# Gate and up of two feed-forward layers as 2x2-block products with seven multiplications in half of their k-groups

## The chip, the cores and the metric

The kernel runs on one core of a Trainium2 chip. The metric is the device time of one execution in microseconds (us). Every matmul operand is float32, split into two float32r parts (high and low), and each product is made of three matmuls: high x high, high x low and low x high.

## What is computed

Two transformer blocks over 256 tokens of width 2048. The change touches their feed-forward layers (FFN), of 5632 hidden columns:

```python
h = h + jnp.concatenate([oa, ob, oc], axis=-1) @ w_out[i]
c = rmsnorm(h, ffn_norm[i])
h = h + conv_ffn(c, w_gate[i], w_up[i], conv_w[i], conv_b[i], w_down[i])
...
x = x + mixed
h = rmsnorm_2(x, ffn_norm_w[l])
x = x + (jax.nn.silu(h @ w_gate[l]) * (h @ w_up[l])) @ w_down[l]
```

`conv_ffn` runs a causal convolution of width 3 along the tokens over the gate's output, adds a bias, takes a gelu and multiplies by the up output, before `w_down`.

## The kernel before

Tokens are two tiles of 128 rows (m = 0, 1). The activations lie transposed as stationary operands: for each of the 16 k-tiles a pair of 128x256 tiles (`xT`, high and low). Weights are the moving operand, in blocks of two k-tiles by 512 columns (128x1024, 512 KB), one block a k-group; `KG` is 2, so a 2048-deep product has eight k-groups.

`load_weight` (L102) gets a block by DMA into one of seven raw buffers (three of tag `raw`, four of tag `t4k`). `split_weight` (L128) makes its parts: ScalarE copies it to `whi` (L133), VectorE subtracts `whi` from the raw block to give `wlo` (L134). `whi` and `wlo` are rings of three buffers. `product` (L158 is the last of its three matmul lines, L156 to L158) runs over the k-groups: a split, then for two k-tiles and two m three matmuls each, 12 in all, into two PSUM banks of tag `acc`. PSUM has four banks of tag `acc` and four of tag `tp`.

An FFN works in units of 512 hidden columns, u = 0 to 10. A unit is `product` with the gate weight and `product` with the up weight, 96 matmuls each; `evacuate` (L236) moves each from PSUM to a `pj` tile of 1024 columns (ring of eight) with the token's factor r. `hidden` turns a unit's result into four pairs of stationary `hid` tiles: transposes on TensorE (L195), then, in the first FFN, five operations on ScalarE and VectorE (L569 to L573) and the split (L184, L185); in the second FFN only the split. These steps are side work: generators in a list, of which `pump` runs up to two steps after each k-group of a product, so that they stand between its matmuls. `ffn` takes units in groups of two, (0, 1) to (8, 9) and (10). After both units of a group the group before is drained: for each of four chunks of 512 columns of h, `product` with the down weight over the group's eight hidden tiles (48 matmuls), then `add_to_h`, two VectorE additions of the banks to h (L544). The last group of the second FFN goes to `final_rows`.

A scheduler orders each engine's row of instructions when the program is built, from the order of the code and its own costs. What stands in `tc.high_priority()`, as the splits do, is put as early as its buffers allow. It also gives out the buffers of a tag. Each engine then runs its row in that order, and an instruction that waits holds all behind it.

`norm_chunk` transposes a chunk of h, scales it by the norm's weights and splits it into `xT`; the token's factor r is applied after the products. In the second block's attention `mod_weights` gets for each head a bias row from DRAM (`vdr`) into one of two `mbias` buffers, after the scores, and adds it there (L838).

Of the kernel before, what the change touches and what calls it, by code (L numbers as in the profile page):

```python
# [17 lines left out]
P = 128  # L18
T = 256
# [34 lines left out]
def two_blocks_kernel(ctx: ExitStack, tc: tile.TileContext, A: dict, out: bass.AP):  # L54
# [87 lines left out]
    def add_side(gen, after=0):  # L142
        side.append([tick[0] + after, gen])
# [54 lines left out]
    def norm_chunk(c, g, st):  # L198

        for kk in range(4):  # L200
            if kk == 2:
                yield 1
            k = c * 4 + kk
            t = transpose_pair([h[c][:, m, kk * P : (kk + 1) * P] for m in range(2)])
            st.xs[k] = stationary(t, "xT", g[:, k : k + 1])
        for m in range(2):
            junk = t2k()
            act(junk, h[c][:, m], AF.Square, accum_out=st.ssq[:, m, c : c + 1])
        if c == NCH - 1:
# [16 lines left out]
    def token_r(st):  # L226
# [4 lines left out]
        pool.tensor_tensor(st.r, ms, mhalf[:, :2], op=ALU.pow)  # L231

# [313 lines left out]
    def residual_norm(w, xin, g, order=None):  # L546

        st = NormState()
# [6 lines left out]
    xs, r = residual_norm(W["out"], mix, G_FFN)  # L555


    def conv_unit(u, xs, r):
        gt = evacuate(product(W["gate"], u, xs), r)
        ut = evacuate(product(W["up"], u, xs), r)  # L560
# [34 lines left out]
    def ffn(unit, down, xs, r, g):  # L595
        groups = [(0, 1), (2, 3), (4, 5), (6, 7), (8, 9), (10,)]
        prev = None
        st = NormState() if g is not None else None

        def drain(u0, hid, last):  # L600
            if last and g is None:
                return final_rows(down, u0, hid)
            for c in range(NCH):
# [11 lines left out]
        drain(*prev, True)  # L615
        return (st.xs, st.r) if g is not None else None
# [59 lines left out]
    def gla_gate(dd):  # L676
        lrt = new([17, T], "lrt", 2)
# [136 lines left out]

    def mod_weights(all_pts, hp):
        (qc, qo), (kc, ko) = mod_at(hp, 0), mod_at(hp, 1)
        qT, kT = t1k(), t1k()
# [12 lines left out]
        for a in range(2):  # L830
            hh = hp * 2 + a
            bt = new([P, 384], "mbias", 2)
            row = vdr[hh : hh + 1, :]
            nc.sync.dma_start(bt, bass.AP(row.tensor, row.offset, [[1, P], [1, 384]]))
# [59 lines left out]
    xs, r = residual_norm(W["out2"], mix, G_FFN2, order=[4, 5, 6, 7, 0, 1, 2, 3])  # L894


    def final_rows(down, u0, hid):
# [3 lines left out]
        tags = [("pj", 8)] * 8 + [("t4k", 4)] * 4 + [("whi", 3)] * 2 + [("wlo", 3)] * 2  # L901
# [150 lines left out]
```

## Time and profile before

| | |
|---|---|
| Median of 3 runs | 2465.67 us (2463.63 to 2466.41) |
| The profiled execution | 2463.04 us |
| Its span in the profile | 2461.1 us, 30001 instructions |
| TensorE, matmuls | 11424, busy 2436.0 us |
| TensorE, weight loads | 11424, busy 2016.2 us |
| VectorE | 1767 instructions, busy 1421.1 us |
| ScalarE | 1705 instructions, busy 1219.0 us |
| DMA | 448.86 MB, mean 182 GB/s |

In a view of the trace a row names the engine (PE is TensorE, PEld its weight loads, DVE VectorE, ACT ScalarE, SP the queue of the DMAs), the line of the code, the operation, and output<-input by the program's tile names with partitions x elements. In square brackets stands how long the engine had been idle before, and what ended it. A matmul's record is longer than the distance to the next one's start, since they are pipelined.

### The profile page before, as it was taken

To read this page: it belongs to the slowest core of one execution; us is meant where nothing else is said; L and a number is where in the kernel's file an instruction comes from. 1 tells how busy PE (TensorE), PEld (TensorE's weight loads), DVE (VectorE), ACT (ScalarE), POOL (GpSimd) and SP (SyncE) were. 2 spreads that over 40 slices of the span, in tenths; PEclk is the share of its full clock that TensorE was granted. 3 is DMA by queue.
4 is the path that set the end of the run, shared out by engine and by line. 5 is a ranking of instruction groups with operands and counts; after the bars stand their busy time and mean duration, and the time that the engine had idled before them with its cause. 6 is when DMAs were issued, how large, how long until landed. Compare 5 with 4: busy or idle time off the path is not lost.

```text
span 2461.1 us, 30001 instructions
## 1 busy us (share of the span) xinstructions
PE 2436.0 (99%) x11424; PEld 2016.2 (82%) x11424; DVE 1421.1 (58%) x1767; ACT 1219.0 (50%) x1705; POOL 20.5 (1%) x26
## 2 busy tenths in 40 slices
PE   8999999999999999999999999999999999999998
PEld 7878888888888888888887888788888888888887
DVE  6686565555556465555656755655545545454556
ACT  6545454455445454544556555654444444434444
POOL 0000000000000000000000000000000000000000
PEclk9999999999999999999999999999999999999999
DMA  7444565555555655555545455555555555555554
GB/s 239 142 144 153 179 205 185 188 187 181 188 190 186 194 182 190 187 188 187 184 150 181 149 198 187 166 162 182 192 189 191 192 189 189 191 192 189 189 195 143
DMA packets 130654, 448.86 MB, mean 182 GB/s; under 512 B 14860, under 2 KB 19852, under 8 KB 130510
## 3 DMA queue, kind: packets, MB, share of 16 engines
q1 hardware_dynamic: 130510, 446.95, 56.2%
q8 instruction: 89, 1.46, 0.2%
q14 instruction: 55, 0.45, 0.1%
HBM read 444.76 MB, written 2.13 MB: 182 GB/s over the span
## 4 chain that ended last, share of the span: by engine, by line
PE 94%; DVE 2%; DMA 1%; issue 1%; ACT 1%; POOL 0%; SPq 0%; POOLq 0%; DVEq 0%; ACTq 0%
PE acc L158 30%; PE acc L156 30%; PE acc L157 29%; PE tp L195 2%; DVE wlo L134 1%; DMA mbias<-vdr 1%; ACT whi L133 0%; PE tp L361 0%; DMA raw<-in_w_down 0%; DMA raw<-in_w_in 0%; PE tp L863 0%; DVE t2k L838 0%; DVE at L370 0%; PE tp L848 0%; DMA h<-in_x 0%
## 5 line engine op out<-in xcount | busy, mean ns | idle before, releaser
L156 PE MATMUL acc<-whi,xT 128*128 128x512 f32 (+3 forms) x2400 | 936.4, 390 | 0.0
L158 PE MATMUL acc<-whi,xT 128*128 128x512 f32 (+3 forms) x2400 | 923.9, 385 | 0.0
L157 PE MATMUL acc<-wlo,xT 128*128 128x512 f32 (+3 forms) x2400 | 923.8, 385 | 0.0
L134 DVE TENSOR_TENSOR wlo<-raw,whi 128x1024 fp32r<-128x1024 f32 (+3 forms) x483 | 575.0, 1191 | 520.0 <-ACT whi L133 519.2
L133 ACT ACTIVATE whi<-raw 128x1024 fp32r<-128x1024 f32 (+3 forms) x483 | 498.9, 1033 | 587.6 <-PE acc L158 526.0
L134 DVE TENSOR_TENSOR wlo<-t4k,whi 128x1024 fp32r<-128x1024 f32 x353 | 432.7, 1226 | 437.0 <-ACT whi L133 436.8
L133 ACT ACTIVATE whi<-t4k 128x1024 fp32r<-128x1024 f32 x353 | 374.3, 1060 | 478.4 <-PE acc L158 458.3
L158 PEld LDWEIGHTS acc<-whi,xT 128*128 128x128 f32 x2400 | 451.1, 188 | 91.0 <-issue 0.9
L156 PEld LDWEIGHTS acc<-whi,xT 128*128 128x128 f32 x2400 | 451.4, 188 | 87.5 <-issue 2.9
L157 PEld LDWEIGHTS acc<-wlo,xT 128*128 128x128 f32 x2400 | 452.0, 188 | 85.6 <-issue 0.4
L156 PE MATMUL acc<-whi,hid 128*128 128x512 f32 x944 | 373.6, 396 | 0.0
L157 PE MATMUL acc<-wlo,hid 128*128 128x512 f32 x952 | 370.8, 389 | 0.0
L158 PE MATMUL acc<-whi,hid 128*128 128x512 f32 x944 | 368.4, 390 | 0.0
L158 PEld LDWEIGHTS acc<-whi,hid 128*128 128x128 f32 x944 | 177.2, 188 | 38.2
L157 PEld LDWEIGHTS acc<-wlo,hid 128*128 128x128 f32 x952 | 179.0, 188 | 35.6
L156 PEld LDWEIGHTS acc<-whi,hid 128*128 128x128 f32 x944 | 177.3, 188 | 35.3 <-issue 0.4
L236 ACT ACTIVATE pj<-acc,r 128x512 f32<-128x512 f32 (+3 forms) x96 | 63.4, 662 | 41.1 <-PE acc L158 41.1
L544 DVE TENSOR_TENSOR h<-h,acc 128x512 f32<-128x512 f32 x104 | 67.1, 680 | 0.0
L195 PE MATMUL tp<-ident,pj 128*128 128x128 f32 x344 | 54.4, 272 | 1.3 <-DVE t2k L838 1.3
L195 PEld LDWEIGHTS tp<-ident,pj 128*128 128x128 f32 x344 | 43.5, 140 | 14.4 <-DVE t2k L838 1.8
L416 ACT ACTIVATE t2k<-t2k,col 128x256 f32<-128x256 f32 (+1 forms) x56 | 26.9, 480 | 23.6 <-DVE col L415 23.5
L184 ACT ACTIVATE hid<-t1k 128x256 fp32r<-128x256 f32 x44 | 18.3, 416 | 35.6 <-DVE t1k L573 35.6
(229 smaller groups left out, 1082.9 us busy)
## 6 DMA issues: line engine op xcount, KB each, us to landing
raw<-in_w_in SPq DMA_DIRECT2D x184, 512.0 KB, 3.5
t4k<-in_w_gate SPq DMA_DIRECT2D x100, 512.0 KB, 3.4
t4k<-in_w_up SPq DMA_DIRECT2D x100, 512.0 KB, 3.4
t4k<-in_w_down SPq DMA_DIRECT2D x96, 512.0 KB, 3.4
raw<-in_w_down SPq DMA_DIRECT2D x80, 512.0 KB, 3.5
raw<-in_w_gate SPq DMA_DIRECT2D x76, 512.0 KB, 3.5
raw<-in_w_up SPq DMA_DIRECT2D x76, 512.0 KB, 3.5
t4k<-in_w_out SPq DMA_DIRECT2D x37, 512.0 KB, 3.5
```

The lines of the kernel that those rows point to most:

```text
L133: act(hi[:, :n], raw[:, :n], AF.Copy)
L134: dve.tensor_tensor(lo[:, :n], raw[:, :n], hi[:, :n].bitcast(F32), op=ALU.subtract)
L156: pe.matmul(o, xhi[:, tok], wh, start=first, stop=False)
L157: pe.matmul(o, xhi[:, tok], wl, start=False, stop=False)
L158: pe.matmul(o, xlo[:, tok], wh, start=False, stop=last)
L184: act(hi, src, AF.Copy)
L195: pe.transpose(t[:, m * P : (m + 1) * P], v, ident)
L236: act(t[:, m, :n], acc[m][:, :n], func, scale=r[:, m : m + 1])
L416: act(lg[:, a:b], lg[:, a:b], AF.Exp, bias=nm[:, m : m + 1], accum_out=sm[:, m : m + 1])
L544: dve.tensor_tensor(h[c][:, m], h[c][:, m], acc[m], op=ALU.add)
```

## The change

Call X the normalized activations and take the weights of gate (a) and up (b) side by side. For a pair of k-groups gp and gp + 4 and the two token tiles, gate and up are a 2x2-block product: b11, b12 are the blocks of gate and up in k-group gp, b21, b22 those in gp + 4. In gp = 0 and 2 of units 2 to 10 (`MIXED`) the eight block products are replaced by seven, in Winograd's form of Strassen's scheme. In gp = 1 and 3, and in units 0 and 1, the eight are kept.

- Weight side: t1 = b11 + b12, t3 = b12 + b22, t2 = t1 + b22, t4 = t2 + b21, each a VectorE addition of 128x1024 written in place into a raw buffer. Split are b11, b21, b22, t1, t3, t2, t4 (`split_raw`): seven where there were four. Each split then feeds six matmuls instead of 12.
- Activation side: `strassen_operands` makes four factors for each of the four k-tiles concerned, once an FFN, as side work; they stay in four of the eight `pj` tiles.
- PSUM: `pair_product` uses all eight banks: p1, q5, p2, q3 of tag `acc`, and q6, q7, x22, q4 of tag `tp`. Beside the fourth group p1, q5, q6 and q7 are combined in two `pj` tiles (ca, cb), and at the end p2, q3, q4 and x22 are added.
- Side work doesn't run inside `pair_product`. `ffn` drains two chunks after each unit instead of four after two units.
- The rings `whi` and `wlo` have five buffers instead of three.
- `norm_chunk` scales the rows of h by the previous norm's factor (rho) before the transposes, where one is given, and r is divided by it.
- `mod_bias` loads the second attention's bias rows at the start of `mod_weights`, into four buffers.

```diff
-        hi, lo = tiles or (new([P, KG * 512], "whi", 3, F32R), new([P, KG * 512], "wlo", 3, F32R))
+        hi, lo = tiles or (new([P, KG * 512], "whi", 5, F32R), new([P, KG * 512], "wlo", 5, F32R))
...
+        if st.rho is not None:
+            rows = [t2k(), t2k()]
+            for m in range(2):
+                act(rows[m], h[c][:, m], AF.Copy, scale=st.rho[:, m : m + 1])
...
+    def strassen_operands(xs):
...
+                    for t, (hi, lo) in ((a, xs[k]), (b, xs[k + 8])):
+                        dve.tensor_tensor(t, hi.bitcast(F32), lo.bitcast(F32), op=ALU.add)
...
+                    dve.tensor_tensor(d, a21, a22, op=ALU.subtract)
+                    dve.tensor_tensor(s2, d, a11, op=ALU.subtract)
+                    dve.tensor_tensor(s3, a11, a21, op=ALU.subtract)
+                    dve.tensor_tensor(s4, s2, a12, op=ALU.add)
+                    x = chunk_tile(F32R)
+                    act(x[:, 0], fm, AF.Copy)
+                    dve.tensor_tensor(x[:, 1], fm, x[:, 0].bitcast(F32), op=ALU.subtract)
...
+    def pair_product(wa, wb, u, xs, sx):
+        p1, q5, p2, q3 = (psum("acc") for _ in range(4))
+        q6, q7, x22, q4 = (psum() for _ in range(4))
+        ca, cb = chunk_tile(), chunk_tile()
...
+        for gp in range(half):
+            if gp not in MIXED:
+                for w_, banks in ((wa, (p2, q4)), (wb, (q3, x22))):
+                    for g in (gp, gp + half):
+                        wt = split_weight(w_, u, g)
+                        for m in range(2):
+                            products(banks[m], plain(g, m), wt, g == KT // KG - 1)
+                continue
+            last = gp == MIXED[-1]
+            b11, b12, b21, b22 = (load_weight(w_, u, g) for g in (gp, gp + half) for w_ in (wa, wb))
+            with tc.high_priority():
+                f11 = split_raw(b11)
+                t1 = b11
+                dve.tensor_tensor(t1, b11, b12, op=ALU.add)
+                f21 = split_raw(b21)
+                f22 = split_raw(b22)
+                t3 = b12
+                dve.tensor_tensor(t3, b12, b22, op=ALU.add)
+            products(p1, plain(gp, 0), f11, last)
+            products(p2, plain(gp + half, 0), f21, gp == half - 1)
+            products(q3, mixed(gp, 3), f22, gp == half - 1)
...
+            products(q5, mixed(gp, 0), ft1, last)
+            products(q7, mixed(gp, 2), ft3, last)
...
+            products(q6, mixed(gp, 1), ft2, last)
...
+            products(q4, plain(gp + half, 1), ft4, gp == half - 1)
+            if last:
+                act(ca[:, 0], p1, AF.Copy)
+                dve.tensor_tensor(ca[:, 1], ca[:, 0], q6, op=add)
+                dve.scalar_tensor_tensor(cb[:, 0], ca[:, 1], -1.0, q5, ALU.mult, add)
+                dve.tensor_tensor(ca[:, 1], ca[:, 1], q7, op=add)
+                dve.tensor_tensor(cb[:, 1], cb[:, 0], q7, op=sub)
+
+        for t, bank in ((ca[:, 0], p2), (cb[:, 0], q3), (ca[:, 1], q4), (cb[:, 1], x22)):
+            dve.tensor_tensor(t, t, bank, op=add)
...
-                add_side(fill(hid, 4 * i, unit(u, xs, r)))
-            if prev is not None:
-                drain(*prev, False)
+                add_side(fill(hid, 4 * i, unit(u, xs, r, sx if u > 1 else None)))
+                if prev is not None:
+                    step = NCH // len(us)
+                    drain(*prev, range(i * step, (i + 1) * step))
...
     def mod_weights(all_pts, hp):
         (qc, qo), (kc, ko) = mod_at(hp, 0), mod_at(hp, 1)
+        bts = [mod_bias(hp * 2 + a) for a in range(2)]
```

What the scheduler made of it, at three places, as rows of an engine (line, operation, output<-inputs). The first is VectorE where the first FFN enters unit 4. Before, the drain's last additions to h stand among splits of the down weight and of the unit's gate weight:

```order
L544 TENSOR_TENSOR h_4_69<-h_4_69,acc_5659 128x512
L134 TENSOR_TENSOR wlo_5775<-t4k_5772,whi_5774 128x1024
L134 TENSOR_TENSOR wlo_5793<-t4k_5790,whi_5792 128x1024
L134 TENSOR_TENSOR wlo_5815<-raw_5812,whi_5814 128x1024
L134 TENSOR_TENSOR wlo_5833<-raw_5830,whi_5832 128x1024
L544 TENSOR_TENSOR h_5_70<-h_5_70,acc_5734 128x512
L544 TENSOR_TENSOR h_5_70<-h_5_70,acc_5735 128x512
```

Now, after the last split of the drain's second chunk; L604 is a split in `split_raw`, L648, L652, L659 and L662 make t1, t3, t2 and t4, L556 is the addition to h, and L700 to L703 and L185 belong to hidden blocks:

```order
L556 TENSOR_TENSOR h_4_69<-h_4_69,acc_5732 128x512
L604 TENSOR_TENSOR wlo_5971<-t4k_5959,whi_5970 128x1024
L701 SCALAR_TENSOR_TENSOR t1k_5840<-tp_5835,cols_82,t1k_5840 128x254
L659 TENSOR_TENSOR t4k_5959<-raw_5953,t4k_5959 128x1024
L604 TENSOR_TENSOR wlo_5994<-raw_5953,whi_5993 128x1024
L662 TENSOR_TENSOR raw_5957<-t4k_5959,raw_5957 128x1024
L703 TENSOR_TENSOR t1k_5840<-t1k_5840,tp_5835 128x256
L604 TENSOR_TENSOR wlo_5999<-raw_5955,whi_5998 128x1024
L185 TENSOR_TENSOR hid_5847<-t1k_5840,hid_5846 128x256
L700 SCALAR_TENSOR_TENSOR t1k_5877<-tp_5872,cols_82,t1k_5877 128x255
L604 TENSOR_TENSOR wlo_6016<-t4k_5959,whi_6015 128x1024
L604 TENSOR_TENSOR wlo_6026<-raw_5957,whi_6025 128x1024
```

Between the first chunk's addition (the first row) and the seventh split now stand sums and hidden operations; the second chunk's additions (h_5) stand six rows below the last one shown.

The second place is TensorE there. Before, the gate's first k-group, 12 matmuls on one split, alternating between two banks:

```order
L156 MATMUL acc_5810<-whi_5814,xT_3518 128x512
L157 MATMUL acc_5810<-wlo_5815,xT_3518 128x512
L158 MATMUL acc_5810<-whi_5814,xT_3519 128x512
L156 MATMUL acc_5811<-whi_5814,xT_3518 128x512
L157 MATMUL acc_5811<-wlo_5815,xT_3518 128x512
L158 MATMUL acc_5811<-whi_5814,xT_3519 128x512
```

Now, from the end of the product with f21 on; tp_5948, tp_5947 and tp_5950 are the banks q7, q6 and q4, and `pj` holds the factors of X:

```order
L624 MATMUL acc_5945<-whi_5966,xT_3898 128x512
L621 MATMUL tp_5948<-whi_5998,pj_4140 128x512
L623 MATMUL tp_5948<-wlo_5999,pj_4140 128x512
L624 MATMUL tp_5948<-whi_5998,pj_4140 128x512
L621 MATMUL tp_5948<-whi_5998,pj_4170 128x512
L623 MATMUL tp_5948<-wlo_5999,pj_4170 128x512
L624 MATMUL tp_5948<-whi_5998,pj_4170 128x512
L621 MATMUL tp_5947<-whi_6015,pj_4140 128x512
L621 MATMUL tp_5950<-whi_6025,xT_3890 128x512
L623 MATMUL tp_5947<-wlo_6016,pj_4140 128x512
```

The products with t3, t2 and t4 follow the one with f21; those with f22 and t1 (banks q3 and q5) were moved behind 17 matmuls of the plain group.

The third place is VectorE in the first FFN's first drain. Before, hidden operations of the last unit alternate with splits and with the drain's additions:

```order
L570 SCALAR_TENSOR_TENSOR t1k_5522<-tp_5517,cols_82,t1k_5522 128x255
L544 TENSOR_TENSOR h_2_67<-h_2_67,acc_5446 128x512
L185 TENSOR_TENSOR hid_5496<-t1k_5489,hid_5495 128x256
L571 SCALAR_TENSOR_TENSOR t1k_5522<-tp_5517,cols_82,t1k_5522 128x254
L134 TENSOR_TENSOR wlo_5623<-t4k_5620,whi_5622 128x1024
```

Now, the end of the hidden operations of units 1 and 2, and what follows:

```order
L703 TENSOR_TENSOR t1k_5294<-t1k_5294,tp_5289 128x256
L185 TENSOR_TENSOR hid_5286<-t1k_5279,hid_5285 128x256
L185 TENSOR_TENSOR hid_5301<-t1k_5294,hid_5300 128x256
L556 TENSOR_TENSOR h_2_67<-h_2_67,acc_5128 128x512
L556 TENSOR_TENSOR h_2_67<-h_2_67,acc_5129 128x512
L556 TENSOR_TENSOR h_3_68<-h_3_68,acc_5324 128x512
L604 TENSOR_TENSOR wlo_5451<-t4k_5410,whi_5450 128x1024
L604 TENSOR_TENSOR wlo_5456<-t4k_5412,whi_5455 128x1024
L556 TENSOR_TENSOR h_3_68<-h_3_68,acc_5325 128x512
```

The additions to h of this drain's first chunk now stand behind eight hidden blocks, and ahead of the splits of t1 and t3 of unit 3.

## Rows read from the trace of the kernel before

**Rows 1.** The page, busy us (share of the span) and instructions of each engine.
```profile
PE 2436.0 (99%) x11424; PEld 2016.2 (82%) x11424; DVE 1421.1 (58%) x1767; ACT 1219.0 (50%) x1705; POOL 20.5 (1%) x26
```

**Rows 2.** Timeline of TensorE in a gate product: start us, us, instruction.
```profile
559.41 0.39 PE L158 MATMUL acc<-whi,xT 128*128 128x512 f32 x1
559.64 0.40 PE L156 MATMUL acc<-whi,xT 128*128 128x512 f32 x1
...
574.84 0.39 PE L157 MATMUL acc<-wlo,xT 128*128 128x512 f32 x1
```

**Rows 3.** The page, shares of the chain that ended last, by engine.
```profile
PE 94%; DVE 2%; DMA 1%; issue 1%; ACT 1%; POOL 0%; SPq 0%; POOLq 0%; DVEq 0%; ACTq 0%
```

**Rows 4.** Windows, one FFN group each: stretch, us, busy by engine, clock, DMA, GB/s.
```profile
656.82:791.34 134.52, 134.52 (x610) 111.24 (x609) 75.71 (x89) 65.13 (x80) 0.00 (x0) 1.00 0.58 188
1922.45:2055.13 132.68, 132.68 (x593) 109.50 (x593) 68.94 (x69) 55.60 (x60) 0.00 (x0) 1.00 0.59 190
```

**Rows 5.** Timeline of VectorE, splits and a hidden block in the first FFN.
```profile
594.26 1.23 DVE L134 TENSOR_TENSOR wlo<-raw,whi 128x1024 fp32r<-128x1024 f32 x1 [1.50 <-ACT whi L133]
595.40 0.48 DVE L570 SCALAR_TENSOR_TENSOR t1k<-tp,cols,t1k 128x255 f32<-128x255 f32 x1
595.92 0.48 DVE L571 SCALAR_TENSOR_TENSOR t1k<-tp,cols,t1k 128x254 f32<-128x254 f32 x1
...
598.62 0.41 DVE L573 TENSOR_TENSOR t1k<-t1k,tp 128x256 f32<-128x256 f32 x1
598.95 0.48 DVE L570 SCALAR_TENSOR_TENSOR t1k<-tp,cols,t1k 128x255 f32<-128x255 f32 x1
599.52 0.42 DVE L185 TENSOR_TENSOR hid<-t1k,hid 128x256 fp32r<-128x256 f32 x1
599.86 0.47 DVE L571 SCALAR_TENSOR_TENSOR t1k<-tp,cols,t1k 128x254 f32<-128x254 f32 x1
```

**Rows 6.** Timeline of ScalarE in a gate product.
```profile
574.13 1.06 ACT L133 ACTIVATE whi<-raw 128x1024 fp32r<-128x1024 f32 x1 [1.66 <-PE acc L158]
576.85 1.06 ACT L133 ACTIVATE whi<-raw 128x1024 fp32r<-128x1024 f32 x1 [1.66 <-PE acc L158]
```

**Rows 7.** Timeline of VectorE, an operation and one that needs its result.
```profile
191.67 1.22 DVE L404 TENSOR_TENSOR t4k<-pj 128x1024 f32<-128x1024 f32 x1
192.92 1.22 DVE L406 TENSOR_REDUCE col<-t4k 128x8 f32<-128x1024 f32 x1
```

**Rows 8.** Timeline of VectorE, two additions to h and the next split.
```profile
656.82 1.28 DVE L544 TENSOR_TENSOR h<-h,acc 128x512 f32<-128x512 f32 x2
658.06 1.23 DVE L134 TENSOR_TENSOR wlo<-raw,whi 128x1024 fp32r<-128x1024 f32 x1
```

**Rows 9.** The page: GB/s of the 40 slices; DMA issues, us to landing.
```profile
GB/s 239 142 144 153 179 205 185 188 187 181 188 190 186 194 182 190 187 188 187 184 150 181 149 198 187 166 162 182 192 189 191 192 189 189 191 192 189 189 195 143
t4k<-in_w_gate SPq DMA_DIRECT2D x100, 512.0 KB, 3.4
raw<-in_w_gate SPq DMA_DIRECT2D x76, 512.0 KB, 3.5
```

**Rows 10.** Timeline of the second attention: TensorE at softmax results, VectorE at a bias.
```profile
1562.26 0.44 PE L195 MATMUL tp<-ident,pj 128*128 128x128 f32 x2 [1.33 <-DVE t2k L838]
1581.91 0.33 PE L848 MATMUL tp<-ident,t2k 128*128 128x128 f32 x1 [1.28 <-DVE t2k L419]
1606.71 0.81 PE L848 MATMUL tp<-ident,t2k 128*128 128x128 f32 x4 [1.04 <-DVE t2k L419]
...
1561.38 0.42 DVE L838 SCALAR_TENSOR_TENSOR t2k<-tp,mbias 128x256 f32<-128x256 f32 x1 [0.68 <-DMA mbias<-vdr]
```

More of the change, by code (lines that the diff above doesn't have):

```diff
@@ L198, in norm_chunk @@
     def norm_chunk(c, g, st):
+        rows = [h[c][:, m] for m in range(2)]
+        if st.rho is not None:
+            rows = [t2k(), t2k()]
+            for m in range(2):
+                act(rows[m], h[c][:, m], AF.Copy, scale=st.rho[:, m : m + 1])
         for kk in range(4):
@@ L203, in norm_chunk @@
             k = c * 4 + kk
-            t = transpose_pair([h[c][:, m, kk * P : (kk + 1) * P] for m in range(2)])
+            t = transpose_pair([rows[m][:, kk * P : (kk + 1) * P] for m in range(2)])
             st.xs[k] = stationary(t, "xT", g[:, k : k + 1])
@@ L231, in token_r @@
         pool.tensor_tensor(st.r, ms, mhalf[:, :2], op=ALU.pow)
+        if st.rho is not None:
+            inv = new([P, 2], "rinv", 2)
+            dve.reciprocal(inv, st.rho)
+            dve.tensor_tensor(st.r, st.r, inv, op=ALU.mult)
     def evacuate(acc, r, n=512, func=AF.Copy, dst=None):
@@ L544, in add_to_h, with residual_norm @@
             dve.tensor_tensor(h[c][:, m], h[c][:, m], acc[m], op=ALU.add)
-    def residual_norm(w, xin, g, order=None):
-        st = NormState()
+    def residual_norm(w, xin, g, rho, order=None):
+        st = NormState(rho)
         for c in range(NCH):
@@ L554, in two_blocks_kernel, with make @@
     ahead[0] = True
[L555 to L560, printed above, removed]
+    xs, r = residual_norm(W["out"], mix, G_FFN, r)
+    def strassen_operands(xs):
+        sx = {}
+        def make():
+            for gp in MIXED:
+                for k in range(gp * KG, gp * KG + KG):
+                    while xs[k] is None or xs[k + 8] is None:
+                        yield 1
+                    yield 1
+                    a, b = t1k(), t1k()
+                    for t, (hi, lo) in ((a, xs[k]), (b, xs[k + 8])):
+                        dve.tensor_tensor(t, hi.bitcast(F32), lo.bitcast(F32), op=ALU.add)
+                    a11, a21, a12, a22 = a[:, :P], a[:, P:], b[:, :P], b[:, P:]
+                    fm = t2k()
+                    d, s2, s3, s4 = (fm[:, i * P : (i + 1) * P] for i in range(4))
+                    dve.tensor_tensor(d, a21, a22, op=ALU.subtract)
[5 more added lines that the diff above has]
+                    dve.tensor_tensor(x[:, 1], fm, x[:, 0].bitcast(F32), op=ALU.subtract)
+                    sx[k] = x
+        add_side(make(), 1)
+        return sx
@@ L562, in hidden, with conv_unit @@
+    def conv_unit(u, xs, r, sx):
+        if sx is None:
+            gt = evacuate(product(W["gate"], u, xs), r)
+            ut = evacuate(product(W["up"], u, xs), r)
+        else:
+            gt, ut = pair_product(W["gate"], W["up"], u, xs, sx)
+            for t in (gt, ut):
+                for m in range(2):
+                    act(t[:, m], t[:, m], AF.Copy, scale=r[:, m : m + 1])
         def hidden(kk):
@@ L598, in ffn, with drain @@
         st = NormState() if g is not None else None
[L600 to L603, printed above, removed]
+        sx = strassen_operands(xs)
+        def drain(u0, hid, chunks, last=False):
+            for c in chunks:
                 add_to_h(c, product(down, c, hid, k0=u0 * 4))
@@ L830, in mod_weights @@
         for a in range(2):
[L831 to L834, printed above, removed]
+            bt = bts[a]
             lg = t2k()
```

71 lines of the change are left out of this document (60 added, 11 removed).

## The prediction, made before the changed kernel had run

> **What bounds the kernel now.** I read the busy times first: TensorE shows 99% of the span, VectorE 58%, ScalarE 50% [rows 1]. A matmul's record overlaps the next one's, so I then read the starts: in a gate product 69 matmuls start between 559.41 and 574.84 us, one every 15.43 / 68 = 0.2269 us, without a hole [rows 2]. The chain of waits agrees: 94% of it is TensorE [rows 3]. Next the period of a whole FFN group (two units of gate and up, then a drain of four chunks). It holds 2 x 192 + 192 = 576 matmuls, which make 130.7 us; the stretch takes 134.52 us in the first FFN and 132.68 in the second [rows 4], and what is over (3.8 us for eight sets of four transposes, 0.48 each) is TensorE work too. VectorE and ScalarE wait there: VectorE stands 1.50 us before a split for ScalarE, and ScalarE 1.66 us for the matmuls that free a ring slot [rows 5, 6]. So the FFN stages, where the change lies, are TensorE's alone, and a matmul less is 0.2269 us less, as long as VectorE still delivers.
>
> **Matmuls removed.** A plain k-group of gate and up (two weights, two block rows) is 48 matmuls; the seven products are 7 x 2 x 3 = 42. Two of the four groups are changed: 12 matmuls a unit. Units 2 to 10 of both FFNs use it: 18 x 12 = 216, and 216 x 0.2269 = 49.0 us. All of them lie on the path.
> The Trainium skill (TensorE: Matmul & The Clock Gate, section "Wait — 56ns, not 53.3ns?") gives 215.7 ns from start to start for 512 columns at full clock; the trace has 226.9 [rows 2], so the measurement decides. By the page the saving would be 216 x 0.2157 = 46.6 us, an estimate.
>
> **VectorE, whole unit.** A mixed group needs seven splits and four sums of 128x1024 there. A split record is 1.23 us, but the next operation starts 1.14 us after it [rows 5], so 1.14 is its price. The trace has no sum of two SBUF blocks with this successor; its bounds are 1.14, and 1.25 for a same-sized operation whose result the next one needs [rows 7]. I take 1.2. So a mixed group costs 7 x 1.14 + 4 x 1.2 = 12.8 us of VectorE against 42 x 0.2269 = 9.5 of TensorE; a plain group 4.6 against 10.9. A unit of the first FFN with its two drain chunks: 30 splits (34.2), 8 sums (9.6), 9 combining operations and 4 additions to h at 0.62 (two take 1.24, [rows 8]; 8.1), four hidden blocks at 0.52 + 0.48 + 0.33 + 0.34 = 1.67 [rows 5] (6.7): 58.6 us. TensorE has 67.26 - 12 x 0.2269 = 64.5. VectorE is at 91%: it fits, if its peaks are covered.
>
> **The cover is the ring of five.** A mixed group is 3.3 us short. Before a drain's end each split holds a slot for 12 matmuls, 2.72 us; with five slots a split may begin four groups, 10.9 us, before its use, and takes 1.06 [rows 6] + 1.23: a lead of 8.5 us, against 3 us with three slots. So 3.3 is covered where VectorE has nothing else. I walked the static orders by hand for the places where it has.
> First FFN, units 4 to 10, first mixed group (the first two order places of the change). Count from the end of the drain's first chunk, for which the addition to h waits. TensorE has 48 matmuls and one set of transposes, 11.2 us, then the products with f11 and f21 until 13.9; the next needs the low part of the split of t3, one matmul later, at 14.1. VectorE stands at that addition at 0 and has until there two additions (1.24), seven hidden operations (2.7), five splits (5.7), four sums (4.8) and some 0.4 of handing over: 14.8. Stall 0.8. The split of t2 comes at 16.8 for 16.4: 0.35. Two products were put behind the plain group because their banks come free with the additions to h of the second chunk, which stand six rows further on, at 23.4 for 23.0: 0.4. With rounding 1.85 us a unit; from the second mixed group on VectorE is ahead again. Seven units: 13 us. Bounds: 0 if ScalarE's and VectorE's orders mesh better, 4 us a unit (28) if every second hand-over costs what the longest hidden chain does.
> First drain of the first FFN (last order place). The tail of unit 1's hidden blocks, formerly made inside the next unit's products, and unit 2's fall into the same two chunks: eight blocks, and the addition to h that frees a bank for unit 3 stands behind all of them. TensorE is done after 96 x 0.2269 + 8 x 0.48 = 25.6 us. VectorE comes to these rows at 7.7 (its third split waits for a slot until then), then 8 x 1.67 + 8 x 1.16 + 0.62 = 23.3: 31.0. Stall 5.4; the third product's bank follows 1.3 late: 6.7, bounds 0 and 12.
> Second FFN: a hidden block is one operation of 0.34, so the same walk ends ahead of TensorE: 0.5 for its first drain, 0.3 for each of eight units, 3 us in all; bounds 0 and 13.
> What the Trainium skill says against this (VectorE: DVE Perf Modes, section "Terms", DRAIN): the next operation can't issue until the pipe is empty. The rows show it starting 0.09 us before the record's end [rows 5]. With 1.23 for 1.14 the walk would end some 1.5 us later in each of seven units, and the sum 11 to 14 us higher.
>
> **Loads.** The sums are written in place and hold four of seven raw buffers until their last split. In the walk each load is issued 6 us or more before its split can begin, and lands in 3.4 to 3.5 us [rows 9]. A mixed group asks for 2.1 MB in 9.5 us, 220 GB/s; the first slice of the span moved 239 [rows 9]. I cost it at nothing; without that cover it is the third rival.
>
> **The rest.** Factors of x (four k-tiles an FFN, some 2.4 us of VectorE each) lie in units 0 and 1, where VectorE is half idle [rows 4]: nothing. Scaling rows by rho before the transposes adds two ScalarE operations to a chain with six k-groups (16 us) of slack: nothing. The bias rows of the second attention are now loaded a step earlier into four buffers. There TensorE stood 1.33, 1.28 and 1.04 us behind softmax operations, and VectorE for the bias load [rows 10]; with that, and splits further ahead, I take 3.7 us back, bounds 0 and 7 (other bursts share the deeper ring). What is late next there is the softmax chain itself.
>
> **Sum.** -49.0 + 13.0 + 6.7 + 3.0 - 3.7 = -30.0 us. The profiled run took 2463.0 us (2.6 below the median), so 2433.0 for a run like it; from the median 2465.67, **2435.7 us**, ratio 0.988. End to end the bounds give -49 - 7 = -56 (2410) and -49 + 28 + 12 + 13 = +4 (2470).
>
> **Rivals.**
> (a) No stalls: the orders mesh and the ring covers everything. -49 - 5 gives 2412. For it: the 8.5 us of lead. Against: additions to h and hidden blocks ahead of the splits in VectorE's row.
> (b) VectorE becomes the bound in the first FFN: 58.6 us of work in a static order with waits in it runs at under 90% filled, and the nine units there keep their 67.3 us; the saving is the second FFN's 24.5 + 3.7 - 3, with 5 lost in the first drain: 2445 to 2450. For it: 91% is much for an engine that waits for ScalarE before nearly each operation.
> (c) Slower: the lead is gone at the start of each mixed group, because a weight block in a held buffer comes late, or slots are held by products that TensorE has put off. Then each of 36 mixed groups runs at VectorE's pace, 3.3 us longer: +119 - 53 = +66, 2531. It decides from 53 / 36 = 1.5 us a group. Against it: loads are 6 us early in the walk, and only the first mixed group of a unit has products put off.
> (d) The change doesn't do what it says: the new products (six matmuls in a row to one bank) run slower than 0.2269. Three in a row already run at it [rows 2]; at 0.25 the 18 x 84 of them cost 35 us, and the sum is near 2470.
>
> **Numbers.** Forecast 0.60, (a) 0.13, (b) 0.19, (c) 0.05, (d) 0.03. The forecast's own spread is 2420 to 2450; with (b) and part of (a) the range is 2414 to 2456. This kernel is measured to about 0.2%, 5 us: faster than 2460.7 in the forecast, (a), (b): 0.92; within 0.2% 0.03; slower 0.05.
>
> **What would show it.** Products of the first FFN's units: 276 a unit with two chunks, a period near 66.4 us in units 4 to 10, and 64 in the second FFN; TensorE holes of about 1 us after the second product of each first mixed group, with VectorE's split named, and one of 5 us at unit 3's start that waits for an addition to h. If there are holes in the second mixed group too, the ring does not cover; if they wait for a load, (c) is right; if matmul starts are further apart than 0.227 inside a product, (d).

## The result, and the profile after

The changed kernel takes **2426.94 us** (median of 4, 2426.54 to 2427.29); the kernel before took 2465.7 us beside it. The ratio is 0.9844, 95% interval 0.9827 to 0.9861. The prediction was 2435.7 us in a range of 2414 to 2456. The profiled run took 2426.8 us with a span of 2425.0, so the spans differ by 36.1 us.

The page of the changed kernel, busy times and the chain's shares by engine, to be read beside [rows 1, 3]:

```profile
span 2425.0 us, 30323 instructions
PE 2392.8 (99%) x11208; PEld 1976.6 (82%) x11208; DVE 1804.9 (74%) x2223; ACT 1352.7 (56%) x1855; POOL 20.8 (1%) x26
...
PE 94%; DVE 3%; issue 1%; ACT 1%; DMA 1%; POOL 0%; SPq 0%; POOLq 0%; DVEq 0%; ACTq 0%
```

There are 11424 - 11208 = 216 matmuls less, TensorE still makes 94% of the chain, and VectorE has gone from 58% to 74%. The windows view gives unit 5 with its two drain chunks, first FFN and second FFN (stretch, then busy us and instructions of TensorE, its weight loads, VectorE, ScalarE and GpSimd, the granted clock, DMA share and GB/s); a group in [rows 4] is two of these:

```profile
749.64:814.20 64.56, 64.56 (x293) 53.25 (x292) 57.56 (x67) 39.17 (x47) 0.00 (x0) 1.00 0.55 196
1991.53:2055.15 63.62, 63.62 (x286) 52.50 (x284) 55.41 (x57) 34.56 (x37) 0.00 (x0) 1.00 0.56 198
```

TensorE is busy in all of both stretches. Half of the old group of the first FFN was 67.26 us and 12 matmuls are 2.72: 64.54 was to be expected without a stall, and units 4 to 9 take 64.57 to 64.61 from first matmul to first matmul. VectorE is 89% busy in the stretch.

To see where 36.1 us went I cut both traces by the starts of TensorE's first matmuls of each stage:

| Stage | before | after | difference | matmuls removed x 0.2269 |
|---|---|---|---|---|
| First attention | 351.9 | 355.8 | +3.9 | |
| Its output projection | 91.4 | 91.4 | 0 | |
| First FFN | 743.75 | 727.58 | -16.2 | -24.5 |
| Between the FFN and the second output projection | 433.7 | 434.5 | +0.8 | |
| Second output projection | 92.2 | 92.2 | 0 | |
| Second FFN to the last matmul | 730.6 | 706.2 | -24.4 | -24.5 |

The second FFN gives all that the matmuls are worth. The first gives 8.3 us less, and the first attention, which the change doesn't touch except through the ring's depth, is 3.9 us longer.

**No stall in units 4 to 10.** The places that the walk was about, unit 5. TensorE, from the unit's first matmul to the product with t3 (`tp<-whi,pj`):

```profile
749.64 0.39 PE L621 MATMUL acc<-whi,xT 128*128 128x512 f32 x1
...
752.13 0.39 PE L624 MATMUL acc<-whi,xT 128*128 128x512 f32 x1
752.36 0.39 PE L621 MATMUL tp<-whi,pj 128*128 128x512 f32 x1
752.58 0.39 PE L623 MATMUL tp<-wlo,pj 128*128 128x512 f32 x1
```

VectorE, from the addition to h of the drain's first chunk to t3's split, the one at 750.93:

```profile
737.76 0.68 DVE L556 TENSOR_TENSOR h<-h,acc 128x512 f32<-128x512 f32 x1
...
740.54 1.22 DVE L648 TENSOR_TENSOR t4k<-t4k,t4k 128x1024 f32<-128x1024 f32 x1
741.68 0.42 DVE L185 TENSOR_TENSOR hid<-t1k,hid 128x256 fp32r<-128x256 f32 x1
...
750.93 1.23 DVE L604 TENSOR_TENSOR wlo<-t4k,whi 128x1024 fp32r<-128x1024 f32 x1
752.07 0.42 DVE L185 TENSOR_TENSOR hid<-t1k,hid 128x256 fp32r<-128x256 f32 x1
```

The split ends at 752.16 and its low part is first used at 752.58: 0.42 us to spare. No row of this place has a wait. What TensorE does before, from the last matmul of the drain's first chunk on:

```profile
737.54 0.39 PE L158 MATMUL acc<-whi,hid 128*128 128x512 f32 x1
737.77 0.60 PE L195 MATMUL tp<-ident,pj 128*128 128x128 f32 x4
...
740.98 0.60 PE L195 MATMUL tp<-ident,pj 128*128 128x128 f32 x4
```

The second chunk holds two sets of transposes, and lasts 749.64 - 737.77 = 11.87 us.

**A stall in the first drain.** The drain lasts 620.48 - 586.88 = 33.6 us; the later two-chunk drains take 23.7. Of the difference 2.0 us are no stall: four more sets of transposes (unit 1's), which stood in unit 2 before. TensorE at the end of its second chunk:

```profile
609.09 0.50 PE L156 MATMUL acc<-whi,hid 128*128 128x512 f32 x1 [1.77 <-ACT hid L184]
...
616.02 0.50 PE L156 MATMUL acc<-whi,hid 128*128 128x512 f32 x1 [3.92 <-ACT hid L184]
...
617.17 0.63 PE L157 MATMUL acc<-wlo,hid 128*128 128x512 f32 x1
617.59 0.63 PE L158 MATMUL acc<-whi,hid 128*128 128x512 f32 x1
...
620.15 0.49 PE L158 MATMUL acc<-whi,hid 128*128 128x512 f32 x1
```

It waits for a hidden tile from ScalarE. ScalarE in turn waits for VectorE (the gelu's input, L701):

```profile
611.62 0.42 ACT L702 ACTIVATE t1k<-t1k 128x256 f32<-128x256 f32 x1 [2.58 <-DVE t1k L701]
```

And VectorE has put unit 3's splits (L604) and sums (L648, L652, L659) ahead of that operation, since they are of high priority:

```profile
604.76 1.22 DVE L648 TENSOR_TENSOR t4k<-t4k,t4k 128x1024 f32<-128x1024 f32 x1
605.90 1.22 DVE L604 TENSOR_TENSOR wlo<-t4k,whi 128x1024 fp32r<-128x1024 f32 x1
607.03 1.22 DVE L652 TENSOR_TENSOR t4k<-t4k,raw 128x1024 f32<-128x1024 f32 x1
...
608.50 1.22 DVE L604 TENSOR_TENSOR wlo<-raw,whi 128x1024 fp32r<-128x1024 f32 x1
...
609.97 1.22 DVE L659 TENSOR_TENSOR raw<-t4k,raw 128x1024 f32<-128x1024 f32 x1
611.10 0.48 DVE L701 SCALAR_TENSOR_TENSOR t1k<-tp,cols,t1k 128x254 f32<-128x254 f32 x1
```

One more sum (L662) follows at 611.50, then VectorE does the rest of the hidden operations until 616.8. The holes of TensorE are 1.77 + 3.92 = 5.7 us. After the second one eight matmuls start 0.43 us apart instead of 0.2269, some 1.6 us more, and the windows view shows the granted clock (the column 0.50) at half, the lower level of 1.2 GHz:

```profile
617.20:620.00 2.80, 2.80 (x8) 2.23 (x7) 1.67 (x3) 1.06 (x1) 0.00 (x0) 0.50 0.00 0
```

Together 7.3 us. Unit 2 with this drain takes 74.4 us, 7.9 more than the 69.25 of experiment 1 less 12 matmuls; some 0.6 of it is in rows without a named wait. The Trainium skill (TensorE: Matmul & The Clock Gate, section "Wait — 56ns, not 53.3ns?") gives 426.7 ns from start to start for 512 columns at 1.2 GHz; the rows agree, (620.15 - 617.17) / 7 = 0.426 us.

### The profile page after: what moved, and what is told of

Read it like the earlier page. It is cut to its first block, busy times and chain, and to the rows that moved or that the text cites. A ratio compares the mean times of both kernels' runs of the same rounds, so it can differ in the third digit from the quotient of the medians.

```text
span 2425.0 us, 30323 instructions
## 1 busy us (share of the span) xinstructions
PE 2392.8 (99%) x11208; PEld 1976.6 (82%) x11208; DVE 1804.9 (74%) x2223; ACT 1352.7 (56%) x1855; POOL 20.8 (1%) x26
## 4 chain that ended last, share of the span: by engine, by line
PE 94%; DVE 3%; issue 1%; ACT 1%; DMA 1%; POOL 0%; SPq 0%; POOLq 0%; DVEq 0%; ACTq 0%
PE acc L156 19%; PE acc L158 19%; PE acc L157 19%; PE acc L621 5%; PE acc L623 5%; PE acc L624 5%; PE tp L623 5%; PE tp L621 5%; PE tp L624 5%; PE tp L195 2%; DVE wlo L134 1%; ACT whi L133 1%; DVE t2k L982 0%; DMA raw<-in_w_down 0%; PE tp L373 0%
## 5 line engine op out<-in xcount | busy, mean ns | idle before, releaser
L134 DVE TENSOR_TENSOR wlo<-raw,whi 128x1024 fp32r<-128x1024 f32 (+3 forms) x421 | 498.0, 1185 | 320.8 <-ACT whi L133 316.2
L133 ACT ACTIVATE whi<-raw 128x1024 fp32r<-128x1024 f32 (+3 forms) x421 | 433.0, 1029 | 417.3 <-PE acc L158 262.5
L156 PE MATMUL acc<-whi,xT 128*128 128x512 f32 (+3 forms) x1248 | 484.3, 388 | 0.0
L157 PE MATMUL acc<-wlo,xT 128*128 128x512 f32 (+3 forms) x1248 | 475.9, 381 | 0.0
L158 PE MATMUL acc<-whi,xT 128*128 128x512 f32 (+3 forms) x1248 | 475.9, 381 | 0.0
L134 DVE TENSOR_TENSOR wlo<-t4k,whi 128x1024 fp32r<-128x1024 f32 x271 | 330.6, 1224 | 175.1 <-ACT whi L133 170.1
L158 PEld LDWEIGHTS acc<-whi,xT 128*128 128x128 f32 x1248 | 235.4, 189 | 45.1 <-issue 0.9
L156 PEld LDWEIGHTS acc<-whi,xT 128*128 128x128 f32 x1248 | 235.6, 189 | 44.1 <-issue 3.2
L157 PEld LDWEIGHTS acc<-wlo,xT 128*128 128x128 f32 x1248 | 235.9, 189 | 42.5 <-DVE wlo L134 1.2
L604 DVE TENSOR_TENSOR wlo<-t4k,whi 128x1024 fp32r<-128x1024 f32 x143 | 173.4, 1222 | 20.3 <-ACT whi L603 18.0
L603 ACT ACTIVATE whi<-raw 128x1024 fp32r<-128x1024 f32 x109 | 115.7, 1062 | 107.8 <-PE acc L158 46.9
L621 PE MATMUL acc<-whi,xT 128*128 128x512 f32 x432 | 168.1, 389 | 0.0
L623 PE MATMUL acc<-wlo,xT 128*128 128x512 f32 x432 | 168.1, 389 | 0.0
L624 PE MATMUL acc<-whi,xT 128*128 128x512 f32 x432 | 168.1, 389 | 0.0
```

Source lines behind the costliest of these rows:

```text
L156: pe.matmul(o, xhi[:, tok], wh, start=first, stop=False)
L157: pe.matmul(o, xhi[:, tok], wl, start=False, stop=False)
L158: pe.matmul(o, xlo[:, tok], wh, start=False, stop=last)
L603: act(hi, raw, AF.Copy)
L604: dve.tensor_tensor(lo, raw, hi.bitcast(F32), op=ALU.subtract)
L621: pe.matmul(bank, shi(j), wh, start=id(bank) not in begun, stop=False)
```

## Experiments

Each is an edit of the changed kernel, or of the one named; ratios are to the kernel before, run beside it. Stage times are cut as in the table above.

**1. Without the seven products.** The eight block products are used in all groups and the factors of X are not made; everything else of the change stays.

```diff
-        sx = strassen_operands(xs)
...
-                add_side(fill(hid, 4 * i, unit(u, xs, r, sx if u > 1 else None)))
+                add_side(fill(hid, 4 * i, unit(u, xs, r, None)))
```

> Every unit takes the ordinary products; the rest of the change stays (rings of five, two drained chunks after each unit, rho, the earlier bias rows). Theory 'the matmuls are the gain': 216 matmuls come back (+49.0 us), the hole in the first drain goes (about -7.5, counting the matmuls at half rate behind it): near 2468 us. Rival 'the rings and the bias rows bring a part': 2455 us or less.

Measured: 2464.64 us, ratio 1.000 [0.9991, 1.0009]. The FFNs take 743.75 and 730.5 us, as before; the first attention takes 355.3, still 3.4 over before. So the matmuls are the whole gain. The deeper rings, the drains of two chunks, rho and the bias rows are worth nothing in sum, and most of the 3.9 us of the first attention has nothing to do with the products. The time is 3 us below the 2468 expected; 2.0 of that lie between the first FFN and the second output projection (432.5 us for 434.5).

**2. Rings of three.**

```diff
-        hi, lo = new([P, KG * 512], "whi", 5, F32R), new([P, KG * 512], "wlo", 5, F32R)
+        hi, lo = new([P, KG * 512], "whi", 3, F32R), new([P, KG * 512], "wlo", 3, F32R)
```

(and so wherever the two tags stand)

> The changed kernel with rings of three for whi and wlo. Theory 'five slots cover VectorE's 3.3 us deficit in a mixed group': with three slots the lead before a mixed group falls from 8.5 to 3 us, and TensorE waits 1 to 3 us in each of 36 mixed groups: 2460 to 2530 us. Rival 'VectorE has room anyway': within 3 us of 2427, or 4 us faster if the deeper rings cost the first attention its 4 us.

Measured: 2507.73 us, ratio 1.0173 [1.0156, 1.0189]: slower than before. One unit of each FFN, windows view:

```profile
688.88:759.53 70.65, 66.70 (x293) 52.90 (x292) 57.98 (x67) 38.82 (x47) 0.00 (x0) 1.00 0.54 179
1979.70:2047.60 67.90, 65.29 (x285) 52.07 (x284) 54.69 (x57) 34.19 (x37) 0.00 (x0) 1.00 0.55 186
```

That is 6.1 and 4.3 us a unit more than with five. TensorE's waits in one unit stand in both mixed groups, most of them at ScalarE's and VectorE's halves of the splits. Four of the six in unit 4 of the first FFN (the other two are 0.38 us for an addition to h and 0.44 for a plain group's split):

```profile
695.50 0.50 PE L621 MATMUL tp<-whi,pj 128*128 128x512 f32 x1 [1.49 <-ACT whi L603]
697.73 0.50 PE L623 MATMUL tp<-wlo,pj 128*128 128x512 f32 x1 [0.57 <-DVE wlo L604]
718.05 0.50 PE L623 MATMUL acc<-wlo,pj 128*128 128x512 f32 x1 [0.26 <-DVE wlo L604]
722.62 0.51 PE L621 MATMUL tp<-whi,xT 128*128 128x512 f32 x1 [0.66 <-ACT whi L603]
```

So the ring is the cover, and without it the price that the prediction gave its slower case comes true: it had 3.3 us a mixed group, 6.6 a unit. The first attention is back at 352.4.

This run also bears on the first drain. Seven of the eight hidden blocks are still transposed in it, but unit 3's first split comes after their last operation on VectorE (L604 at 612.88, L185 at 611.94). TensorE's waits in this drain are then short:

```profile
602.73 0.73 PE L156 MATMUL acc<-whi,hid 128*128 128x512 f32 x2 [0.47 <-ACT whi L133]
603.98 0.50 PE L156 MATMUL acc<-whi,hid 128*128 128x512 f32 x1 [0.52 <-ACT hid L184]
```

TensorE waits in unit 3's first mixed group instead, 2.44 and 1.73 us for splits where the later units have 1.49 and 0.57.

**3. Hidden blocks early.** Before unit 2 all side work that is left is issued, so that unit 1's hidden blocks don't fall into the first drain.

```diff
             for i, u in enumerate(us):
+                while u == 2 and side:
+                    pump()
                 add_side(fill(hid, 4 * i, unit(u, xs, r, sx if u > 1 else None)))
```

> Before unit 2 the side steps left over from unit 1 (its hidden blocks) are put ahead of unit 2's products, in both FFNs. Theory 'the hole stands in the order, four hidden blocks too many in the first drain': the holes of 1.77 and 3.92 us and the half-rate matmuls go, up to 1.5 us come in for transposes that wait for unit 1's result: 2420 us. Rival 'VectorE lacks the time in the drain wherever the blocks stand': 2426 to 2428.

Measured: 2419.88 us, ratio 0.9815 [0.9801, 0.983]. The first FFN takes 720.03 us, 7.55 less and within 0.8 of 743.75 - 24.5. In the first drain TensorE has no idle time left (windows view):

```profile
588.00:612.00 24.00, 24.00 (x115) 19.81 (x114) 19.41 (x26) 13.35 (x20) 0.00 (x0) 1.00 0.35 115
```

**4. One sum more.** An operation that changes nothing, after t3 in each mixed group: 36 more of 128x1024, some 41 us of VectorE.

```diff
                 dve.tensor_tensor(t3, b12, b22, op=ALU.add)
+                dve.tensor_tensor(t3, t3, t3, op=ALU.max)
```

> One more VectorE operation of 128x1024 (1.14 us) in each mixed group, ahead of the sum t2. Theory 'margin of 0.4 us in the first FFN's first mixed groups, more elsewhere': 0.7 us in each of 7 units and 1 to 2 in the first drain, +7 us: 2434. Rival 'VectorE is the bound': 36 x 1.14 = +41 us: 2468. Rival 'room everywhere': 2427 to 2429.

Measured: 2437.65 us, ratio 0.9893 [0.9878, 0.9908], 10.7 us more. The profiled execution took 2442.17, the longest of the four, and is 15.4 us over the changed kernel's: 10.4 in the first FFN, 1.4 in the second and 3.6 outside the FFNs. Units 4 to 9 of the first FFN take 65.9 us each (64.6 without), with one hole a unit in the first mixed group:

```profile
691.07 0.50 PE L621 MATMUL tp<-whi,pj 128*128 128x512 f32 x1 [0.90 <-ACT whi L603]
```

```profile
689.96 1.06 ACT L603 ACTIVATE whi<-t4k 128x1024 fp32r<-128x1024 f32 x1 [0.34 <-PE acc L624]
```

The matmul is the first of the product with t2, and what it waits for is ScalarE's half of t2's split, which itself waited 0.34 us for a ring slot. The scheduler set another order with the extra operation: the product with f21, which stood ahead of t3's and t2's, now stands behind them, so that TensorE asks for them six matmuls earlier. So this run doesn't measure VectorE's margin of 0.42. What it shows is that no second mixed group has a hole, that the first drain takes 1.2 us more and the second FFN has one hole of 0.97 us, at an addition to h of its first drain, and that VectorE, with 41 us more to do, is not the bound.

**5. Rings of four**, with the hidden blocks early.

```diff
-        hi, lo = new([P, KG * 512], "whi", 5, F32R), new([P, KG * 512], "wlo", 5, F32R)
+        hi, lo = new([P, KG * 512], "whi", 4, F32R), new([P, KG * 512], "wlo", 4, F32R)
```

(and so wherever the two tags stand)

> As early hidden blocks, rings of four instead of five. Theory: a slot less takes 2.7 us of lead. Second mixed groups stay covered (5.8 us of lead for 3.3 short), the first mixed groups of units 4 to 10 of the first FFN, which have about 0.4 us to spare, lose up to 2.3 us each, 16 us in all, and the second FFN next to nothing: 2425 to 2437. Rival: the loss goes with the number of slots (rings of three cost 81 us over five in the same kernel otherwise), so half of it, 2460.

Measured: 2442.25 us, ratio 0.9907 [0.989, 0.9923]. Units 4 to 9 of the first FFN take 66.84 us each, 2.24 more, as expected (2.3), by two holes in the first mixed group alone, both at low parts of splits:

```profile
681.61 0.50 PE L623 MATMUL tp<-wlo,pj 128*128 128x512 f32 x1 [0.76 <-DVE wlo L604]
683.88 0.50 PE L623 MATMUL tp<-wlo,pj 128*128 128x512 f32 x1 [0.61 <-DVE wlo L604]
```

The first is where the walk had looked, the low part of the first split behind the product with f21. The total lies 5 us over the range expected: the second FFN, which I had put at next to nothing, loses 9.7 us (0.6 a unit, and 4.7 in unit 2 with one hole of 3.17), and units 2 and 3 of the first lose 5.1 besides, while the stages outside the FFNs give 7.5 back. The loss does not go with the number of slots. The fifth is worth 2442.25 - 2419.88 = 22 us in all and 30.5 in the FFNs alone; the fourth is worth 2507.73 - 2442.25 = 65.5, a few us of which are the early hidden blocks, which experiment 2 hasn't (its unit 3 takes 74.4 us where the later ones take 70.6).

**6. Two slots for the FFNs alone**, hidden blocks early; the two are tags of their own, used by the fourth and fifth of every five splits.

```diff
+    def split_tiles():
+        more = in_ffn[0] and next(slots) % 5 > 2
+        return tuple(new([P, KG * 512], t + "_f", 2, F32R) if more else new([P, KG * 512], t, 3, F32R) for t in ("whi", "wlo"))
```

> As early hidden blocks, but five split slots only inside the two FFNs: the rings keep three buffers in the attentions and projections, and two further buffers are used by the FFNs' splits alone. Theory: the deeper rings are what cost the first attention 3.5 us (355.8 and 355.3 us with five, 352.4 with three, 351.9 before); with three there it is back near 352, FFNs as with five (720.0 and 706.3), the total 2416. Rival: the first attention's loss comes from other edits or from how the scheduler happens to place things: 2420 or more.

Measured: 2438.28 us, ratio 0.9893 [0.9879, 0.9908]. The attentions did what the theory says (352.5 and 328.9 us), but the first FFN takes 746.0 instead of 720.0, with holes of 1.15 and 0.53 us in the plain group of each unit from 3 on. In units 5 to 9 the granted clock is at its lower level behind them, for some seven matmuls, and the unit takes 68.4 us where units 3 and 4 take 66.9 with the same two holes:

```profile
754.17:756.73 2.56, 2.56 (x8) 2.00 (x6) 0.59 (x1) 0.00 (x0) 0.00 (x0) 0.50 0.92 366
```

With two tags a split is bound to one of them when the code is written, and the scheduler set another order. The total expected was missed by 22 us; the part of the theory on the attentions held, and whether the first FFN could have kept its time with slots of its own this run doesn't settle.

**7. and 8. Two slots held**, hidden blocks early. The ring stays one of five; idle tiles hold two slots in the attention and let go of them when its last column block is there. Once in the first attention, once in both.

```diff
+    def hold():
+        tiles = [new([P, KG * 512], t, 5, F32R) for t in ("whi", "wlo") for _ in range(2)]
+        for t in tiles:
+            dve.memset(t[:, :1].bitcast(F32), 0.0)
+        return tiles
...
+            dve.tensor_tensor(t[:, :1], t[:, :1].bitcast(F32), late, op=ALU.max)
...
+    held = hold()
...
+    let_go(held, c13[:, 0, :1])
     xs, r = residual_norm(W["out"], mix, G_FFN, r)
```

> As early hidden blocks with rings of five, but two of the five slots are held by idle tiles during the first attention and given back before its output projection, so that the feed-forward layers keep one ring of five in the scheduler's order. Theory: five slots cost the first attention what three do not, 3.5 us (2.0 in the run of early hidden blocks): first attention 352, first feed-forward layer 720, total 2416 to 2418. Rival: what undid the version with two extra slots (26 us in the first feed-forward layer) is any change of the ring ahead of it: 2440.

> The same with two slots held in the second attention too. Theory: second attention 329 us (it was 328.9 in three runs with three slots there and 329.5 to 334.1 in four with five), so 2 to 5 us less again: 2412 to 2415. Rival: no further gain there, 2416 to 2418.

Measured: 2415.34 us, ratio 0.9801 [0.9785, 0.9817], and **2413.48 us**, ratio 0.9791 [0.9776, 0.9805], the fastest of all. FFNs 720 and 706.3 in both. Against experiment 3 the span of 7 is 5.9 us shorter: 2.0 in the first attention, as expected, and 3.9 between the first FFN and the second output projection, where nothing was held; why, no run shows. Experiment 8 has 0.9 less again in the second attention; its 1.9 us in all are less than the intervals tell apart. The attentions by slots, all runs (the second from its first matmul to the output projection):

| Slots | first attention | second attention |
|---|---|---|
| 3 (before) | 351.9 | 330.8 |
| 3, or 5 with two held | 352.4, 352.5, 352.6, 352.4, 352.1 | 328.9, 328.9, 328.9, 329.2 |
| 4 | 351.5 | 329.4 |
| 5 | 355.8, 355.3, 354.4, 357.9, 356.1 | 331.6, 329.5, 334.1, 333.1, 331.5, 330.2 |

So with five slots the first attention takes 2 to 5.5 us more and the second up to 5. With three the second takes 1.9 less than before (330.8 to 328.9); the earlier bias rows are the likely cause, but no run has them alone. Where five slots lose is seen in the first attention. ScalarE in the changed kernel, then TensorE:

```profile
142.52 0.60 ACT L359 ACTIVATE t4k<-tp 128x512 f32<-128x512 f32 x1 [2.11 <-PE tp L358]
...
143.56 1.28 ACT L474 ACT_TABLE_LOAD   x1
144.86 0.21 ACT L474 ACTIVATE lfa<-lfa 128x12 f32<-128x12 f32 x1
145.09 1.28 ACT L359 ACT_TABLE_LOAD   x1
146.38 0.60 ACT L359 ACTIVATE t4k<-tp 128x512 f32<-128x512 f32 x1
```

```profile
147.03 0.50 PE L357 MATMUL tp<-cm,pj 128*128 128x512 f32 x1 [2.44 <-ACT t4k L359]
```

The second exponential of an attention head stands behind a logarithm (L474) with a table load before and after, and TensorE waits 2.44 us for it. With two slots held both exponentials go ahead of the logarithm, and that hole isn't there (L370 and L485 are the same lines):

```profile
137.34 0.60 ACT L370 ACTIVATE t4k<-tp 128x512 f32<-128x512 f32 x1 [2.09 <-PE tp L369]
138.01 1.06 ACT L133 ACTIVATE whi<-raw 128x1024 fp32r<-128x1024 f32 x1
...
139.08 0.58 ACT L370 ACTIVATE t4k<-tp 128x512 f32<-128x512 f32 x1
139.68 1.28 ACT L485 ACT_TABLE_LOAD   x1
```

So this hole comes from the order that the scheduler built with the deeper ring, in a stage with table loads in it. It is one hole of several; that the rest of the loss is of this kind is not shown.

**9. and 10. The seven products in unit 1 too**, with the hidden blocks early (9), and with the two tags of experiment 6 besides (10).

```diff
+                while u == 1 and len(sx) < 4:
+                    pump()
-                add_side(fill(hid, 4 * i, unit(u, xs, r, sx if u > 1 else None)))
+                add_side(fill(hid, 4 * i, unit(u, xs, r, sx if u > 0 else None)))
```

> As early hidden blocks, and unit 1 of each FFN has the seven products too; the factors of x are made before it. Theory: 2 x 12 matmuls less at 0.2269 us is 5.4 us, if the factors and unit 0's hidden blocks stay beside TensorE's work: 2414.5. Rival: VectorE is late with the factors at unit 1's start or the side work of unit 0 piles up: 2420 or more.

> Early hidden blocks, five split slots in the FFNs alone, and the seven products in unit 1 too. If the last two act as their theories say and independently, 2419.9 - 3.5 - 5.4 = 2411. If one of them doesn't, 2414 to 2416; if neither, 2420.

Measured: 2426.08 us, ratio 0.9841 [0.9826, 0.9855], and 2427.94, ratio 0.9852 [0.9837, 0.9867]: no gain, 6 and 8 us over the early hidden blocks alone. In 9 the first FFN has 7.9 us more (727.96) instead of 2.7 less. Unit 1 takes 41.2 us, 5.7 less than in experiment 3, but unit 2 takes 55.3 before its drain, 13.6 more. Side work doesn't run inside the seven products, so unit 0's hidden blocks, which ran inside unit 1's products, now fall with unit 1's at the start of unit 2, eight blocks in a row. TensorE waits there for VectorE's hidden operations:

```profile
555.27 0.95 PE L195 MATMUL tp<-ident,pj 128*128 128x128 f32 x7 [2.13 <-DVE t1k L703]
558.83 0.66 PE L195 MATMUL tp<-ident,pj 128*128 128x128 f32 x4 [2.06 <-DVE t1k L703]
560.28 0.50 PE L621 MATMUL tp<-whi,pj 128*128 128x512 f32 x1 [0.79 <-DVE t1k L703]
```

Behind them the granted clock is 0.50 from 561.68 to 564.24. So the rival, side work that piles up, is what happened, one unit later than it said. The independent gains expected of 10 did not add up either. In its first FFN (734.1 us) units 4 to 9 took 65.1 to 65.7 us and not the 66.9 to 68.5 of experiment 6, with the same two tags; that it hangs on which of the splits come fourth and fifth is likely, not shown.

## Why the prediction was right, and which of its steps were not

| Step | predicted, us | measured, us |
|---|---|---|
| 216 matmuls | -49.0 | -49.0 by count; -24.4 of -24.5 in the second FFN |
| Units 4 to 10, first FFN | +13.0 | +0.4 (7 x 0.06) |
| First drain, first FFN | +6.7 | +7.6 (experiment 3) |
| Second FFN | +3.0 | +0.1 |
| Second attention | -3.7 | +0.8 |
| First attention | not in the sum | +3.9 |
| Sum | -30.0 | -36.2; the spans say -36.1 |

- **Matmuls.** Right in count and price. The new products run at the old pace: in the rows of unit 5 above, 749.64 to 752.58 is 13 distances of 0.226 us from start to start. The rival of slower products falls.
- **VectorE's load.** 58.6 us of 64.5 were worked out; the windows row shows 57.56 of 64.56. The sums were taken at 1.2 us; L648 above starts 1.14 before its successor. The rival that VectorE is the bound in the first FFN kept the units at 67.3 us; they take 64.6, with VectorE 89% busy and no wait of TensorE.
- **Units 4 to 10: the step that failed.** The walk put the end of t3's split 14.8 us behind its zero point, the end of the drain's first chunk, and the need for its low part at 14.1. In the trace the chunk ends at 737.77, the first addition to h starts at 737.76, the split ends 752.16 - 737.76 = 14.4 later and its low part is used after 752.58 - 737.77 = 14.8. VectorE was over-priced by 0.4, half of it the sums. The larger error, 0.7, is TensorE's side: the walk gave the second chunk 48 matmuls and one set of transposes, and it holds two sets (rows 737.77 and 740.98), 0.49 us more. The walk's own sum was short as well: 48 x 0.2269 + 0.48 is 11.4 and not 11.2; the chunk takes 11.87. A stall of 0.8 was the small difference of two sums of 14 us, and an error of 1.1 turned it into a margin of 0.42. The term was also larger than its parts: 0.8 + 0.35 + 0.4 is 1.55, and the 1.85 a unit that went into the sum put 2 us more on seven units. That the place is tight was right: experiment 5, with a slot less, opens a hole just there.
- **The Trainium skill against the walk.** By the Trainium skill (VectorE: DVE Perf Modes, section "Terms", DRAIN) the walk would have ended later and the sum 11 to 14 us higher. The trace goes the other way: where the next operation waits for nothing, sums, like splits, are followed after 1.13 to 1.14 us, before their record's 1.22 ends.
- **First drain: right size, other place.** To take four of the eight hidden blocks out gives 7.55 us back. But the eight alone don't make the hole: with rings of three (experiment 2) the waits in this drain are 0.5 us each. And TensorE doesn't wait at unit 3's start for an addition to h. It waits inside the drain's last chunk for hidden tiles, since unit 3's splits, for which the deeper ring has slots free, and sums went in front of them on VectorE. The walk let VectorE do the hidden blocks first, as though the row were in the code's order there. The 1.6 us of low clock behind the hole were not in it.
- **Ring of five.** Right as the cover (experiments 2 and 5), with the price of the slower case at 6.1 and 4.3 us a unit for the 6.6 worked out. What it costs elsewhere was looked for only in the second attention, as a bound. There -3.7 became +0.8: the second attention takes 1.9 less than before with three slots, and five took more than that away. The first attention lost 3.9. Experiments 7 and 8, which hold two slots there, give 6.4 us back (2419.88 to 2413.48).
- **Loads, factors, rho at nothing.** Right: down weights now take 5.1 us to land and gate weights up to 4.2, over the 3.4 to 3.5 of [rows 9], but TensorE's waits in the FFNs of the changed kernel name no load.

By the terms the sum is 6.2 us lower than forecast: 15.5 us of stalls that weren't there, against 8.4 of attention that was not foreseen and 0.9 of the drain. The other 2.6 of the 8.8 us between forecast and median are the distance of the profiled run before from its median; the profiled run after lies at its own.

That the forecast came within 9 us is in part luck. In the units of both FFNs the rival of no stalls is what happened; the 8.4 us of the attentions that the forecast didn't have made up for half of the 15.5 us of stalls that weren't there. The first drain's size came out near by another wait than the one worked out. What was right by its own working is the saving by the matmuls, and that the ring covers VectorE.

## What to carry to other kernels

Fewer matmuls pay in full on a TensorE-bound stage as long as another engine's extra work has a deep enough ring in front of it; price the cover by taking a slot away, since here the last one was worth 22 us (30 in the FFNs alone) and the one before it some 60. When a hand walk ends within a few per cent of its own length, say "tight", not "stall", and count the side work of both engines in the stretch: one set of transposes missed on TensorE was most of the error here. A shared ring or a priority changes the order in stages that the change never meant, so look for its price there, and at what the high-priority work displaces just ahead of a group's first unit.

## What was not expected of the hardware

- After TensorE's hole of 3.92 us the granted clock was at its lower level: eight matmuls 0.43 us apart, 0.50 granted in 617.20 to 620.00, and 1.00 again in the window 620.40 to 626.00. Ahead of that hole, behind one of 1.77 us, it had stayed at 1.00. A long hole isn't needed: in experiment 6 holes of 1.15 and 0.53 us within 3 us were followed by 0.50 in units 5 to 9 (754.17 to 756.73 in unit 5), and the same two holes in units 3 and 4 were not. So in these rows the length of a hole alone doesn't tell whether the clock falls.
- Two table loads of ScalarE (1.28 us each) around one logarithm of 12 columns (0.21 us) made TensorE wait 2.44 us. In this stage the order on ScalarE cost more than its load, since the engine is busy for only 196 of the 356 us from 8.5 to 364.5.
